# A mixed prompt and decode step: where the decode rows' attention takes its cached values from

## The chip, the cores and the metric

One core of one Trainium2 chip runs the whole program in one launch. The metric is the device time of that core in microseconds (us); of several runs the median is taken. The profile comes from one further execution of the same kernel.

## What is computed

A decoder trunk of two layers, all in float32, for a prompt of 512 tokens and for 8 sequences in decoding with 4 new tokens each (32 rows). Layer 0 is a convolution module and a SwiGLU feed-forward ("FFN0"). From its output one shared K/V is projected, and layer 1 attends with it in three branches (compressed, selected, window) and ends with a second feed-forward. For the decode rows the past 1024 tokens of the selected branch lie in a paged cache, and the page table says which page of 128 tokens is whose:

```python
def gather_pages(cache, page_table):
    g = cache[page_table]
    return g.reshape(page_table.shape[0], page_table.shape[1] * PAGE_SIZE, *cache.shape[2:])
...
sel_full = jnp.concatenate([gather_pages(cache_kv_sel, page_table), rows[:, :, 1]], axis=1)
...
blk_k, blk_v = selection_blocks(sel_full)
...
s_s = jnp.einsum('bqgrd,bgqksd->bgqksr', q, ks).astype(jnp.float32) + bias_s
p_s = masked_softmax(s_s.reshape(B, KV_HEADS, Q, nk, GROUP), smask.reshape(B, KV_HEADS, Q, nk)[..., None], 3)
o_s = jnp.einsum('bgqnr,bgqnd->bqgrd', p_s.astype(vs.dtype), vs.reshape(B, KV_HEADS, Q, nk, HEAD_DIM))
```

A token of `cache_kv_sel` is 2 KB: keys of 4 heads of 64 numbers (1 KB), then the values of the same heads (1 KB). `cache_kv_win` (512 past tokens a sequence) is laid out alike and not paged.

## The kernel before

The program is one stream of Python generators. TensorE (PE) does the matrix products, mostly as three passes over high and low halves of float32 numbers (`whi`, `wlo`, `h_hi`, `h_lo`, lines 183 and 185). The order of instructions on each engine is chosen at build time by a scheduler with a timing model of its own; on the chip every engine works through its own list strictly in order, and so do the DMA queues of SP (SyncE, where weights are loaded) and of POOL (GpSimd). Work with no hurry is handed to a long stage as `between` steps and is mixed into it.

Five pieces matter here:

- `setup` builds row tables from the page table: for each partition and sequence the row of the cache to fetch (`rows4`, four tables, lines 384 to 387).
- `key_steps` (lines 1289 to 1309) is mixed into FFN0. For each of 8 sequences and 3 chunks of 512 tokens (two of the paged cache, one of the window) it fetches the chunk into `kr`, transposes its keys on DVE (VectorE) into `ktr` (line 1304, two instructions a chunk) and writes them to a DRAM scratch `kt_d` with SP (line 1307, four writes). A paged chunk comes by one indirect DMA on POOL (`load_rows`, line 1030): 128 rows of 8 KB, each with four tokens' keys and values. The values half goes on to a second DRAM scratch, `v_d`, by one SP write of 512 KB (line 1299). `kr` has two buffers.
- `decode_attention(pool, gp)` (lines 1312 to 1461) runs for each of two pairs of heads, `gp`, and in it for two sets `st` of four sequences. Scores against the compressed keys (line 1324) and against `kt_d` (line 1379) go through the softmax (line 1346); the probabilities are transposed and multiplied with the values (line 1443, `b<-vs,pT`): for each chunk and sequence four products with 128 values each. Values stand in `vs` tiles, one per chunk and sequence, in 8 buffers. SP loads them from `v_d` (line 1434, 32 loads of 256 KB) and from the window cache (line 1436).
- `decode_rows` (lines 1182 to 1186) and `keys_values` (lines 1226 and 1231) write new rows out through POOL's DMA queue; `keys_values` is the projection of the prompt's shared K/V, and its products stand beside the decode attention on PE. `compressed_branch` (line 1558) stands behind them.
- `prompt_attention` comes next; its first product with probabilities is line 1530 (`o<-pTp,vn`). It takes over the PSUM banks that the decode attention used.

The values' way before, in lines 1299 and 1434:

```python
self.load_rows(kr.rearrange("p t e -> p (t e)"), A["cache_kv_sel"], 2 + c, b)
self.sy.dma_start(self.v_d[b, c].rearrange("(p t) d -> p t d", t=4), kr[:, :, 256:])
...
self.sy.dma_start(vb, self.v_d[bb[b], c].rearrange("(a p) d -> p a d", p=P)[:, :, gp * P:(gp + 1) * P])
```

Of the kernel before, what the change touches and what calls it, by code (L numbers as in the profile page):

```python
# [14 lines left out]
P = 128  # L15
# [3 lines left out]
NB = 8  # L19
# [45 lines left out]
def shape_constants():  # L65
# [22 lines left out]
    c["kbase"] = (p % 32).astype(f)[:, None]  # L88
    pages = np.arange(8)[:, None, None] == np.stack([p % 32 // 4, p // 32, 4 + p // 32])
    c["iota"] = np.broadcast_to(np.arange(16, dtype=f), (P, 16))  # L90
    names, cols, at = [], [], 0
# [22 lines left out]
class Kernel:  # L114
# [187 lines left out]
    def setup(self, sp):  # L302
# [46 lines left out]
        self.g.dma_start(ptab, A["page_table"].rearrange("b j -> j b"))  # L349
        ptf = sp.tile([8, NB], F32, name="ptf")  # L350

# [31 lines left out]
        for i in range(3):  # L383
            self.te.matmul(pt[:, i * NB:(i + 1) * NB], pages[:, i * P:(i + 1) * P], ptf, start=True, stop=True)
        for i, col in enumerate((self.cbase[:, 0:1], self.cbase[:, 1:2], self.kbase, self.kbase)):
            j = max(i - 1, 0)
            self.v.tensor_scalar(self.rows4[:, i], pt[:, j * NB:(j + 1) * NB], col, None, op0=ALU.add)
        pt = self.bank()
# [638 lines left out]
    def load_rows(self, out, cache, i, b):  # L1027

        src = cache.rearrange("n (k t) e g d -> (n k) (t e g d)", t=4)
        self.g.indirect_dma_start(out=out, out_offset=None, in_=src, in_offset=bass.IndirectOffsetOnAxis(ap=self.rows4[:, i, b:b + 1], axis=0))  # L1030

# [255 lines left out]


    def key_steps(self, pool):


        A = self.A
        winc = A["cache_kv_win"].rearrange("b (p t) e g d -> p b t (e g d)", t=4)
        for b in range(NB):
            for c in range(3):
                kr = pool.tile([P, 4, 512], F32, name="kr", bufs=2)
                if c < 2:
                    self.load_rows(kr.rearrange("p t e -> p (t e)"), A["cache_kv_sel"], 2 + c, b)
                    self.sy.dma_start(self.v_d[b, c].rearrange("(p t) d -> p t d", t=4), kr[:, :, 256:])
                else:  # L1300
                    self.sy.dma_start(kr[:, :, :256], winc[:, b, :, 0:256])
                kt = pool.tile([P, 2, 4, P], F32, name="ktr", bufs=2)
# [9 lines left out]
    def decode_attention(self, pool, gp):  # L1312
        A, v, s, g, te = self.A, self.v, self.s, self.g, self.te
        bs = pool.tile([P, SK], F32, name="bs1")
        self.sy.dma_start(bs, self.bs_d[gp].unsqueeze(0).broadcast_to([4, 32, SK]))
        winc = A["cache_kv_win"].rearrange("b (c p) e g d -> p b c (e g d)", p=P)
        for st in range(2):
            bb = range(4 * st, 4 * st + 4)
# [98 lines left out]
            for c in range(4):  # L1417
# [11 lines left out]
                if c < 3:  # L1429
                    vs = []  # L1430
                    for b in range(4):
                        vb = pool.tile([P, 4, P], F32, name="vs", bufs=8)
                        if c < 2:
                            self.sy.dma_start(vb, self.v_d[bb[b], c].rearrange("(a p) d -> p a d", p=P)[:, :, gp * P:(gp + 1) * P])
                        else:
                            self.sy.dma_start(vb, winc[:, bb[b], :, 256 + gp * P:256 + (gp + 1) * P])
                        vs.append(vb)
# [7 lines left out]

            od = pool.tile([P, 2, HD], F32, name="od", bufs=2)
            t0 = pool.tile([P, HD], F32, name="t0", bufs=1)
# [198 lines left out]
    def run(self):  # L1646
# [5 lines left out]
        with sbuf("const") as self.cp, sbuf("norm") as self.np, \  # L1652
# [9 lines left out]
            self.kt_d = dp.tile([NB, 3, 2, P, 512], F32, name="kt_d")  # L1662
            self.v_d = dp.tile([NB, 2, 512, 256], F32, name="v_d")
            self.vtail = dp.tile([NB, 40, 256], F32, name="vtail")
            self.rows4 = cp.tile([P, 4, NB], I32, name="rows4")
            self.cks = cp.tile([P, NB, 2, 32], F32, name="cks")
# [148 lines left out]
```

## Time and profile before

| what | value |
|---|---|
| time, median of 3 runs | 1660.17 us (1652.02 to 1661.15) |
| the profiled execution's own time | 1661.26 us |
| its span in the trace | 1659.5 us |
| PE (TensorE matmul) busy | 1555.0 us, 94% |
| DVE (VectorE) busy | 1107.8 us, 67% |
| ACT (ScalarE) busy | 694.1 us, 42% |
| POOL (GpSimd) busy | 235.2 us, 14% |
| DMA moved | 295.26 MB, mean 178 GB/s |

How to read it: times in the trace count from the start of the span. A busy PE counts its matmuls from start to modelled end. "Idle before" an instruction is the time its engine did nothing, put down to what ended it. A DMA's duration on POOL or SP is the time that it holds that queue's engine; when its bytes have landed is told apart. The DMA share of a stretch is the mean busy share of the core's 16 DMA engines.

### The profile page before, as it was taken

To read this page: it belongs to the slowest core of one execution; us is meant where nothing else is said; L and a number is where in the kernel's file an instruction comes from. 1 tells how busy PE (TensorE), PEld (TensorE's weight loads), DVE (VectorE), ACT (ScalarE), POOL (GpSimd) and SP (SyncE) were. 2 spreads that over 40 slices of the span, in tenths; PEclk is the share of its full clock that TensorE was granted. 3 is DMA by queue.
4 is the path that set the end of the run, shared out by engine and by line. 5 is a ranking of instruction groups with operands and counts; after the bars stand their busy time and mean duration, and the time that the engine had idled before them with its cause. 6 is when DMAs were issued, how large, how long until landed. Compare 5 with 4: busy or idle time off the path is not lost.

```text
span 1659.5 us, 31626 instructions
## 1 busy us (share of the span) xinstructions
PE 1555.0 (94%) x12423; PEld 1366.8 (82%) x12423; DVE 1107.8 (67%) x2369; ACT 694.1 (42%) x1443; POOL 235.2 (14%) x270
## 2 busy tenths in 40 slices
PE   6897998999988889999999899999999999999997
PEld 3784677989978878999977677655699999999997
DVE  2897866482447788576657644867856865874865
ACT  5321115242222344255445422755746542552554
POOL 3444401021220112001110000000011110110010
PEclk9898979999999999999999999999999999999999
DMA  9577575374399999834779895746122472333231
GB/s 307 140 200 155 151 241 168 117 227 130 112 241 312 299 303 325 247 103 106 184 228 306 245 282 183 237 148 229 52 68 73 152 233 84 91 114 90 79 91 64
DMA packets 315568, 295.26 MB, mean 178 GB/s; under 512 B 16019, under 2 KB 275485, under 8 KB 311179
## 3 DMA queue, kind: packets, MB, share of 16 engines
q1 hardware_dynamic: 304507, 237.24, 48.7%
q0 software_dynamic: 10224, 55.47, 10.7%
q8 instruction: 98, 1.61, 0.4%
q10 hardware_dynamic: 688, 0.53, 0.1%
q14 instruction: 51, 0.42, 0.1%
HBM read 256.28 MB, written 45.48 MB: 182 GB/s over the span
## 4 chain that ended last, share of the span: by engine, by line
PE 65%; DMA 13%; DVE 10%; issue 6%; SPq 2%; ACT 2%; POOL 1%; ACTq 0%; DVEq 0%; POOLq 0%
PE g L185 18%; PE g L183 17%; PE g L247 8%; DMA raw<-in_w_down_dram 4%; PE t L247 3%; PE t L155 3%; PE o L1530 2%; DMA raw<-in_w_ada_dram 2%; DVE wlo L196 2%; PE t L1049 2%; PE a L452 1%; PE t L1379 1%; PE t L730 1%; PE sc L1509 1%; DVE y L768 1%
## 5 line engine op out<-in xcount | busy, mean ns | idle before, releaser
L169 ACT CAST whi<-raw 128x512 fp32r<-128x512 f32 x250 | 149.7, 606 | 408.7 <-PE g L185 280.1
L170 DVE TENSOR_TENSOR wlo<-raw,whi 128x512 fp32r<-128x512 f32 x250 | 173.0, 696 | 156.5 <-ACT whi L169 155.6
L183 PE MATMUL g<-h_hi,whi 128*128 128x256 f32 (+1 forms) x584 | 170.5, 293 | 13.9 <-DVE un L680 9.3
L185 PE MATMUL g<-h_hi,whi 128*128 128x288 f32 (+4 forms) x584 | 173.5, 298 | 0.9 <-ACT h_hi L575 0.9
L185 PE MATMUL g<-h_hi,wlo 128*128 128x288 f32 (+4 forms) x584 | 173.9, 298 | 0.0
L185 PE MATMUL g<-h_lo,whi 128*128 128x288 f32 (+4 forms) x584 | 173.7, 297 | 0.0
L183 PE MATMUL g<-h_lo,whi 128*128 128x256 f32 (+1 forms) x584 | 168.3, 288 | 3.0 <-DVE h_lo L830 3.0
L183 PE MATMUL g<-h_hi,wlo 128*128 128x256 f32 (+1 forms) x584 | 167.3, 287 | 0.0
L183 PEld LDWEIGHTS g<-h_hi,whi 128*128 128x128 f32 x584 | 111.5, 191 | 27.3 <-issue 16.2
L247 PE MATMUL g<-T,whi 128*128 128x272 f32 x656 | 127.9, 291 | 4.1 <-DVE sg L261 2.5
L195 ACT CAST whi<-s 128x512 fp32r<-128x512 f32 x128 | 79.1, 620 | 99.9 <-PE g L247 61.7
L183 PE MATMUL g<-a_hi,whi 128*128 128x256 f32 (+1 forms) x372 | 108.0, 291 | 12.4 <-ACT ht L912 4.3
L183 PEld LDWEIGHTS g<-h_lo,whi 128*128 128x128 f32 x584 | 111.8, 192 | 8.0 <-issue 4.3
L185 PEld LDWEIGHTS g<-h_hi,whi 128*128 128x128 f32 x584 | 111.3, 191 | 4.2 <-issue 2.9
L185 PEld LDWEIGHTS g<-h_hi,wlo 128*128 128x128 f32 x584 | 111.3, 191 | 2.6 <-issue 2.5
L185 PEld LDWEIGHTS g<-h_lo,whi 128*128 128x128 f32 x584 | 111.2, 190 | 2.6 <-issue 2.5
L183 PEld LDWEIGHTS g<-h_hi,wlo 128*128 128x128 f32 x584 | 111.5, 191 | 1.8 <-issue 1.7
L196 DVE TENSOR_TENSOR wlo<-s,whi 128x512 fp32r<-128x512 f32 x128 | 89.1, 698 | 34.0 <-ACT whi L195 32.2
L185 PE MATMUL g<-a_hi,wlo 128*128 128x288 f32 (+1 forms) x372 | 111.1, 299 | 0.0
L185 PE MATMUL g<-a_hi,whi 128*128 128x288 f32 (+1 forms) x372 | 110.9, 299 | 0.0
L185 PE MATMUL g<-a_lo,whi 128*128 128x288 f32 (+1 forms) x372 | 110.7, 298 | 0.0
L247 PEld LDWEIGHTS g<-T,whi 128*128 128x128 f32 x656 | 103.8, 190 | 5.6 <-ACT whi L195 2.2
(511 smaller groups left out, 4165.2 us busy)
## 6 DMA issues: line engine op xcount, KB each, us to landing
raw<-in_w_ada_dram SPq DMA_DIRECT2D x84, 512.0 KB
raw<-in_w_gate_dram SPq DMA_DIRECT2D x44, 512.0 KB
raw<-in_w_up_dram SPq DMA_DIRECT2D x44, 512.0 KB
raw<-in_w_down_dram SPq DMA_DIRECT2D x32, 512.0 KB
raw<-in_w_pw_dram SPq DMA_DIRECT2D x24, 512.0 KB
kt_d<-ktr SPq DMA_DIRECT2D x96, 128.0 KB
kt<-kt_d SPq DMA_DIRECT2D x24, 512.0 KB
raw<-in_w_kv_dram SPq DMA_DIRECT2D x20, 512.0 KB
```

Source lines behind the costliest of these rows:

```text
L155: self.te.transpose(out, in_, self.ident[:n, :n])
L169: self.s.copy(hi[:, :b - a], raw[:, a:b])
L170: self.v.tensor_tensor(out=lo[:, :b - a], in0=raw[:, a:b], in1=hi[:, :b - a].bitcast(F32), op=ALU.subtract)
L183: self.te.matmul(pg[:, 0, :split], a, b[:, i, :split], start=st, stop=sp)
L185: self.te.matmul(pg[:, 1, :tokens - split], a, b[:, i, split:tokens], start=st, stop=sp)
L195: self.s.copy(hi, src)
L196: self.v.tensor_tensor(out=lo, in0=src, in1=hi.bitcast(F32), op=ALU.subtract)
L247: self.te.matmul(out, a[:, i], b(i), start=first and i == 0 and j == 0, stop=i == 3 and j == 2, skip_group_check=not first)
L452: self.te.matmul(pa[32 * j:32 * j + 32, :256], self.cT[:, k, :], w[:, j * 256:(j + 1) * 256], start=k == 0, stop=k == KT - 1)
L730: self.te.matmul(pt[32 * gg:32 * gg + 32], wds[q // 4][:, gg, q % 4], vs[:, gg, 4 * q:4 * q + cols], start=q == 0, stop=q == 7)
L1049: te.matmul(ph[:, :P], self.w1[:, e, c // 2, c % 2], xv[:, c % 2, c // 2], start=c == 0, stop=c == 15)
L1530: te.matmul(po[rp * HD:(rp + 1) * HD, :256], self.vn[:, br, t, gg * HD:(gg + 1) * HD], pT[:, rp * 256:(rp + 1) * 256], start=br == 0 and t ...
```

## The change

The values are no longer fetched with the keys, nor kept in `v_d`, which is gone.

- In `key_steps` a paged chunk comes by four indirect DMAs in place of one, each with 128 rows of 1 KB: the keys of one token per partition. The table `rowsk` (four small DVE instructions) holds their rows. `kr` is half as large and has four buffers. The write to `v_d` is dropped.
- In `decode_attention` each `vs` tile of a paged chunk is filled by four indirect DMAs on POOL, each with 128 rows of 512 B (the values of one token for one pair of heads): 64 for each `gp`, 128 in all, in place of 32 loads on SP. Their table `rowsv` is made for each `gp` by eight small products with the page table and one DVE instruction. `od` has one buffer in place of two.
- `rows4` shrinks to two tables; `rowk` and the page table in float32 (`ptf`) stay in SBUF. One more transposition of `vb` into a bank of its own stands in `setup`; nothing reads it.

```diff
@@ setup
-        for i, col in enumerate((self.cbase[:, 0:1], self.cbase[:, 1:2], self.kbase, self.kbase)):
-            j = max(i - 1, 0)
-            self.v.tensor_scalar(self.rows4[:, i], pt[:, j * NB:(j + 1) * NB], col, None, op0=ALU.add)
+        for i in range(2):
+            self.v.tensor_scalar(self.rows4[:, i], pt[:, :NB], self.cbase[:, i:i + 1], None, op0=ALU.add)
+        self.v.tensor_scalar(self.rowk.rearrange("p c b -> p (c b)"), pt[:, NB:3 * NB], self.kbase, None, op0=ALU.add)
+        pt = self.bank()
+        self.transpose(pt[:, :66], vb)
@@ 
+    def gather(self, out, rows, at):
+        self.g.indirect_dma_start(out=out, out_offset=None, in_=rows, in_offset=bass.IndirectOffsetOnAxis(ap=at, axis=0))
@@ key_steps
+        rows = pool.tile([P, 4, 2, NB], I32, name="rowsk")
+        for t in range(4):
+            self.v.tensor_scalar(rows[:, t], self.rowk, 8.0, 2.0 * t, op0=ALU.mult, op1=ALU.add)
         for b in range(NB):
             for c in range(3):
-                kr = pool.tile([P, 4, 512], F32, name="kr", bufs=2)
+                kr = pool.tile([P, 4, 256], F32, name="kr", bufs=4)
                 if c < 2:
-                    self.load_rows(kr.rearrange("p t e -> p (t e)"), A["cache_kv_sel"], 2 + c, b)
-                    self.sy.dma_start(self.v_d[b, c].rearrange("(p t) d -> p t d", t=4), kr[:, :, 256:])
+                    for t in range(4):
+                        self.gather(kr[:, t], A["cache_kv_sel"].rearrange("n t e g d -> (n t e) (g d)"), rows[:, t, c, b:b + 1])
                 else:
-                    self.sy.dma_start(kr[:, :, :256], winc[:, b, :, 0:256])
+                    self.sy.dma_start(kr, winc[:, b, :, 0:256])
@@ decode_attention
+        pt = self.bank("ds")
+        for j in range(8):
+            te.matmul(pt[:, j * NB:(j + 1) * NB], self.ident[:8, j:j + 1].broadcast_to([8, P]), self.ptf, start=True, stop=True)
+        rows = pool.tile([P, 8, NB], I32, name="rowsv")
+        v.tensor_scalar(rows.rearrange("p j b -> p (j b)"), pt[:, :8 * NB], self.vrow[:, 0:1], self.vrow[:, gp + 1:gp + 2], op0=ALU.mult, op1=ALU.add)
...
                         if c < 2:
-                            self.sy.dma_start(vb, self.v_d[bb[b], c].rearrange("(a p) d -> p a d", p=P)[:, :, gp * P:(gp + 1) * P])
+                            for j in range(4):
+                                self.gather(vb[:, j], A["cache_kv_sel"].rearrange("n t e (h g) d -> (n t e h) (g d)", h=2),
+                                            rows[:, 4 * c + j, bb[b]:bb[b] + 1])
...
-            od = pool.tile([P, 2, HD], F32, name="od", bufs=2)
+            od = pool.tile([P, 2, HD], F32, name="od", bufs=1)
@@ run
-            self.v_d = dp.tile([NB, 2, 512, 256], F32, name="v_d")
```

The build-time order moves with it, at three places. The first is POOL's list while the keys are fetched (`kr` are the keys, `a_lo` the low half of an FFN0 activation that PE reads), before:

```order
L1030 DMA kr<-in_cache_kv_sel_dram,rows_78 128x2048 x2
L920 TENSOR_TENSOR a_lo<-ht,a_hi 128x544
L1030 DMA kr<-in_cache_kv_sel_dram,rows_78 128x2048
L920 TENSOR_TENSOR a_lo<-ht,a_hi 128x544
L1030 DMA kr<-in_cache_kv_sel_dram,rows_78 128x2048 x7
L984 TENSOR_TENSOR a_lo<-ht,a_hi 128x544
```

and after:

```order
L1037 DMA kr<-in_cache_kv_sel_dram,rowsk 128x256 x12
L924 TENSOR_TENSOR a_lo<-ht,a_hi 128x544
L1037 DMA kr<-in_cache_kv_sel_dram,rowsk 128x256 x12
L924 TENSOR_TENSOR a_lo<-ht,a_hi 128x544
L1037 DMA kr<-in_cache_kv_sel_dram,rowsk 128x256 x40
L988 TENSOR_TENSOR a_lo<-ht,a_hi 128x544
```

Twelve gathers stand where two and one stood, and all 64 come before the third `a_lo` shown here; before, six of the 16 came behind it.

The second place is POOL's list in the decode attention (`vs` are the value gathers, `rows` the decode rows written out, `row`, `vn` and `acc` the rows that `keys_values` writes out). Before it holds no `vs`:

```order
L1164 TENSOR_TENSOR hs<-hs,rstd 128x256
L1182 DMA out_dram<-rows 32x256
L1184 DMA out_dram<-rows 4x256 x8
L1182 DMA out_dram<-rows 32x256
L1184 DMA out_dram<-rows 4x256 x8
L1186 DMA vtail<-rows 8x4x256 x2
L1226 DMA out_dram<-row 128x4x256 x2
L1231 DMA out_dram<-acc 32x512
L1226 DMA out_dram<-row 128x4x256
L1226 DMA out_dram<-vn 128x4x256
L1226 DMA out_dram<-row 128x4x256
L1226 DMA out_dram<-vn 128x4x256
```

and after, from the last write of the decode rows on (15 gathers stand ahead of the first of these writes):

```order
L1193 DMA vtail<-rows 8x4x256 x2
L1037 DMA vs<-in_cache_kv_sel_dram,rowsv 128x128 x17
L1233 DMA out_dram<-row 128x4x256
L1037 DMA vs<-in_cache_kv_sel_dram,rowsv 128x128 x32
L1233 DMA out_dram<-row 128x4x256
L1238 DMA out_dram<-acc 32x512
L1037 DMA vs<-in_cache_kv_sel_dram,rowsv 128x128 x32
L1233 DMA out_dram<-row 128x4x256
L1233 DMA out_dram<-vn 128x4x256
L1037 DMA vs<-in_cache_kv_sel_dram,rowsv 128x128 x32
L1233 DMA out_dram<-row 128x4x256
L1233 DMA out_dram<-vn 128x4x256
```

The 128 gathers come as 15, 17, 32, 32 and 32, with the 20 writes of the decode rows behind the first 15, and one or two of the writes of `keys_values` between the later groups; one `row` and one `vn` stand just ahead of the last 32.

The third place is PE's list at the end of the decode attention (`vs,pT` are the products with the values, `g<-` those of `keys_values`, `ht,zk` those of the compressed branch). Before, the last values are followed by 288 passes `g<-` ahead of line 1530:

```order
L1443 MATMUL b<-vs,pT 32x128 x14
L1443 MATMUL b<-vt,pT 32x128 x4
L183 MATMUL g<-h_hi,whi 128x256
L185 MATMUL g<-h_hi,whi 128x256
L183 MATMUL g<-h_lo,whi 128x256
```

and after by 96:

```order
L1461 MATMUL b<-vs,pT 32x128 x16
L157 MATMUL a<-c_small,tl 40x128
L1461 MATMUL b<-vs,pT 32x128 x32
L1461 MATMUL b<-vt,pT 32x128 x4
L157 MATMUL b<-c_small,od 128x128
L1576 MATMUL b<-ht,zk 32x512 x4
```

So 192 passes of `keys_values` moved ahead of the last products with values; the compressed branch's eight products stand behind them in both.

## Rows read from the trace of the kernel before

**Rows 1.** the page's first lines: busy time, share and instructions of each engine

```profile
PE 1555.0 (94%) x12423; PEld 1366.8 (82%) x12423; DVE 1107.8 (67%) x2369; ACT 694.1 (42%) x1443; POOL 235.2 (14%) x270
```

**Rows 2.** windows: length, busy us (count) of PE, PEld, DVE, ACT, POOL, PEclk, DMA share, GB/s

```profile
460.00:660.00 200.00, 176.72 (x1336) 164.36 (x1335) 146.29 (x244) 70.65 (x137) 30.53 (x27) 0.95 0.99 298
...
580.00:620.00 40.00, 35.05 (x264) 31.80 (x263) 32.66 (x53) 16.68 (x33) 6.11 (x5) 0.96 1.00 304
620.00:660.00 40.00, 36.53 (x286) 32.79 (x285) 34.93 (x57) 19.49 (x39) 8.51 (x7) 1.00 1.00 317
...
780.00:820.00 40.00, 35.71 (x280) 34.96 (x279) 23.82 (x58) 19.76 (x40) 6.17 (x12) 1.00 0.85 188
...
820.00:1060.00 240.00, 229.49 (x2037) 181.60 (x2036) 142.15 (x438) 101.38 (x231) 17.62 (x31) 0.99 0.81 243
```

**Rows 3.** DMA of the stretch 460 to 700 us

```profile
DMA packets 80561, 70.78 MB, mean 295 GB/s; under 512 B 3368, under 2 KB 76034, under 8 KB 78493
```

**Rows 4.** line 1304, the key transpositions on DVE: ns min/median/max, first and last start

```profile
L1304 DVE STREAM_TRANSPOSE ktr<-kr x48: 1053/1094/1147, 482.5 to 684.4; 128x512 f32<-128x512 f32 x48
```

**Rows 5.** POOL in order of time, at the first key gathers

```profile
473.32 1.05 POOL L1030 DMA_INDIRECT kr<-in_cache_kv_sel_dram,rows  x1 [11.97 <-DMA line_f<-lsb]
474.67 0.97 POOL L1030 DMA_INDIRECT kr<-in_cache_kv_sel_dram,rows  x1 [0.30 <-issue]
475.67 1.36 POOL L920 TENSOR_TENSOR a_lo<-ht,a_hi 128x544 fp32r<-128x544 f32 x1
```

**Rows 6.** PE's instructions on tile a_lo, 470 to 510 us

```profile
L183 PE MATMUL g<-a_lo,whi x16: 275/282/415, 486.8 to 509.8; 128*128 128x256 f32 x16
```

**Rows 7.** the chain of waits, 780 to 1080 us: start, us, what

```profile
785.83 19.34 DMA raw<-in_w_down_dram
```

**Rows 8.** SP in order of time, 780 to 812 us

```profile
786.24 19.76 SPq L1434 DMA_DIRECT2D vs<-v_d  x6
```

**Rows 9.** line 1030, the gathers on POOL

```profile
L1030 POOL DMA_INDIRECT kr<-in_cache_kv_sel_dram,rows x16: 936/973/1468, 473.3 to 658.3; - x16
...
DMA to landing us min/median/max: 5.6/8.5/10.6
```

**Rows 10.** line 1324, the first products of the decode attention

```profile
L1324 PE MATMUL t<-cks,qz x32: 196/206/217, 856.1 to 946.5; 128*32 128x32 f32 x32
```

**Rows 11.** POOL in order of time, 820 to 1060 us

```profile
863.49 0.57 POOL L1182 DMA_DIRECT2D out_dram<-rows  x1 [32.91 <-ACT rows L1175]
...
875.44 1.18 POOL L1186 DMA_DIRECT2D vtail<-rows  x2
930.19 0.81 POOL L1226 DMA_DIRECT2D out_dram<-row  x1 [53.57 <-ACT row L132]
...
988.09 0.79 POOL L1226 DMA_DIRECT2D out_dram<-row  x1 [24.65 <-DVE row L134]
1006.22 0.75 POOL L1226 DMA_DIRECT2D out_dram<-vn  x1 [17.34 <-DVE vn L134]
```

**Rows 12.** line 1443, the products with the values, and what PE waited for there

```profile
L1443 PE MATMUL b<-vs,pT x384: 272/273/421, 885.5 to 988.0; 128*32 128x128 f32 x192
L1443 PE MATMUL b<-vt,pT x32: 269/281/293, 900.8 to 988.3; 40*32 40x128 f32 x32
...
  DMA vs<-in_cache_kv_win_dram: 1.2, 3
```

**Rows 13.** the chain of waits: one batch of 34 products with values

```profile
987.18 1.41 PE b L1443 x34
```

**Rows 14.** line 1530, the prompt attention's products with probabilities

```profile
L1530 PE MATMUL o<-pTp,vn x320: 379/379/431, 1048.5 to 1218.3; 128*64 128x256 f32 x160
```

**Rows 15.** PE in order of time, two passes of keys_values

```profile
1002.34 0.28 PE L183 MATMUL g<-h_hi,whi 128*128 128x256 f32 x1
1002.46 0.28 PE L185 MATMUL g<-h_hi,whi 128*128 128x256 f32 x1
```

**Rows 16.** plain DMAs on POOL, mean duration

```profile
L1184 POOL DMA_DIRECT2D out_dram<-rows x16 | 8.2, 519 | 2.6 <-DMA out_dram<-rows 2.4
```

More of the change, by code (lines that the diff above doesn't have):

```diff
@@ L89, in shape_constants @@
     pages = np.arange(8)[:, None, None] == np.stack([p % 32 // 4, p // 32, 4 + p // 32])
+    c["vrow"] = np.stack([512 + 0 * p, 4 * p + 2, 4 * p + 3], 1).astype(f)
     c["iota"] = np.broadcast_to(np.arange(16, dtype=f), (P, 16))
@@ L349, in setup @@
         self.g.dma_start(ptab, A["page_table"].rearrange("b j -> j b"))
-        ptf = sp.tile([8, NB], F32, name="ptf")
+        ptf = self.ptf
         self.s.activation(c9, c9, AF.Silu)
@@ L1029, in load_rows @@
         src = cache.rearrange("n (k t) e g d -> (n k) (t e g d)", t=4)
-        self.g.indirect_dma_start(out=out, out_offset=None, in_=src, in_offset=bass.IndirectOffsetOnAxis(ap=self.rows4[:, i, b:b + 1], axis=0))
+        self.gather(out, src, self.rows4[:, i, b:b + 1])
+    def gather(self, out, rows, at):
+        self.g.indirect_dma_start(out=out, out_offset=None, in_=rows, in_offset=bass.IndirectOffsetOnAxis(ap=at, axis=0))
     def compress_steps(self, pool):
@@ L1662, in run @@
             self.kt_d = dp.tile([NB, 3, 2, P, 512], F32, name="kt_d")
-            self.v_d = dp.tile([NB, 2, 512, 256], F32, name="v_d")
             self.vtail = dp.tile([NB, 40, 256], F32, name="vtail")
-            self.rows4 = cp.tile([P, 4, NB], I32, name="rows4")
+            self.rows4 = cp.tile([P, 2, NB], I32, name="rows4")
+            self.rowk = cp.tile([P, 2, NB], F32, name="rowk")
+            self.ptf = cp.tile([8, NB], F32, name="ptf")
             self.cks = cp.tile([P, NB, 2, 32], F32, name="cks")
```

## The prediction

> **What bounds the kernel now.** I read the page's busy times first. PE is busy 94% of the span, POOL 14% [rows 1]: POOL has room on average, but an average says nothing of one stage. So the second view is busy time by windows [rows 2]. Two stretches matter. From 460 to 660 us the keys are fetched beside FFN0: PE is busy 176.72 of 200 us at a mean granted clock of 0.95, and the DMA share stands at 0.99. That stretch is held back by transfers, by 200 - 176.72 = 23.3 us at most, and by the clock as well. From 820 to 1060 us (decode rows, decode attention, projection of the shared K/V) PE is busy 229.49 of 240 us, so PE is the bound there, and POOL is busy just 17.62 us. The wait list of the value products shows PE waiting three times, 1.2 us in all, for values of the window and not for those of the scratch [rows 12]: the loads that the change takes away cost PE nothing there. The third view is the chain of waits. Just before, at 785.83, it runs for 19.34 us through a load of `w_down` [rows 7], while SP's list shows six early value loads issued right behind it over 19.76 us [rows 8]; PE loses 40 - 35.71 = 4.3 us in that window [rows 2].
>
> **The change, part by part.**
>
> *Fetching keys: a gain.* The gathers shrink from 16 x 128 x 8 KB = 16.8 MB to 64 x 128 x 1 KB = 8.4 MB, and the writes to `v_d`, 16 x 512 KB = 8.4 MB, go. That is 16.8 of the 70.78 MB that move from 460 to 700 us [rows 3], 24%. It isn't 24% of the time: PE can get back only its idle time. Moreover the new order draws the key transpositions together: where they stood in 48 places from 482.5 to 684.4 us [rows 4], all 64 gathers now stand ahead of an `a_lo` that had six of 16 behind it. The first part of the stretch therefore stays full of transfers and the last part becomes free. I take PE's idle time of the last two windows, 40 - 35.05 and 40 - 36.53, together 8.4 us [rows 2].
>
> Against that, POOL's list puts 12 gathers ahead of the `a_lo` that stood behind two. A gather holds POOL 0.973 us in the median [rows 9], and 0.30 us passes before the next [rows 5]: **1.27 us each**. From 473.32 the 12 end at 488.6, `a_lo` with its 1.36 us at 490.0 [rows 5]; PE first reads it at 486.8 [rows 6]. Cost 3.2 us. The six early loads of values vanish from SP, so I count the 4.3 us at 785 as gained. **Lead** when the decode attention starts: 8.4 + 4.3 - 3.2 = 9.5 us. Its ends: all idle time and the clock back is 23.3 + 4.3 + 5% of 176.72, 36 us; with gathers at 1.77 us (the longest, 1.468, and the gap) the `a_lo` would be some 10 us late and nothing gained, -10 us.
>
> *Fetching values: a loss.* 128 gathers now stand in POOL's list, where none was. The trace has none with rows of 512 B. The nearest row is the key gather: also 128 rows, on the same queue, but 16 times the bytes. From below I bound it by a plain DMA on POOL, 0.52 us [rows 16], from above by 1.77 us. I take 1.27 us, since number of rows and kind of instruction agree and only the bytes differ. Row and gap show that gathers are not run one after another: the second started 1.35 us behind the first [rows 5], though one takes 8.5 us until its data has landed [rows 9].
>
> The Trainium skill, "DMA: Bandwidth & Descriptors", section "Anatomy of one DMA", fits a DMA from this queue by 2.0 us plus bytes over 436 GB/s, which is 2.15 us for 64 KB (an estimate from the page); one after the other, 128 would hold the queue 275 us, and the sum below would be near 1790 us. By the two rows just given the fixed part overlaps, so the trace speaks against adding it up.
>
> Now the queue, step by step. The index table hangs on products that stand just ahead of line 1324, which started at 856.1 [rows 10]; less the lead, 846.6. Fifteen gathers: 865.7. The decode rows' 20 writes hold POOL from 863.49 to 876.62 [rows 11], 13.1 us: 878.8. Seventeen gathers: 900.4. One `row`, 0.81: 901.2. Thirty-two: 941.8. Two small writes, 1.6: 943.4. Thirty-two: 984.1; `row`, 0.8: 984.9. Next stands `vn`, and it isn't ready: it was at 1006.22 [rows 11], so 996.7 now, and what is queued behind it, the last 32 gathers, waits 12 us with it. With its 0.75 us: 997.5. Thirty-two gathers: 1038.1. The last, issued at 1036.8, lands 8.5 us later: 1045.3. Its 36 products take 1.5 us, as 34 took 1.41 [rows 13]: **1046.8**, where the last one before ended at 988.6 [rows 12]. So the values, which SP had ready in time, become the last thing to arrive, by 58 us. The eight buffers of `vs` hold 32 gathers, 41 us of the queue, so they don't add a wait.
>
> *What PE does meanwhile.* PE isn't idle for 58 us: 192 passes of `keys_values` moved ahead of the last value products. At 0.12 us a pass (1002.34 to 1002.46) [rows 15] that is 23.0 us of work no longer behind them. Before, 1048.5 - 988.3 = 60.2 us lay between the last value product and the prompt attention's first product with probabilities [rows 12, 14]; now 60.2 - 23.0 = 37.2 us, since the compressed branch and the remaining passes still stand behind and the prompt attention takes over the banks. It comes at 1046.8 + 37.2 = 1084.0, 35.5 us late.
>
> *The small edits* cost nothing that counts: the index tables, 16 products of eight columns and six DVE instructions in all, and the dead transposition are under a microsecond each and lie beside transfers; without that cover they would add some 3 us. `od` with one buffer is reused tens of microseconds later. Transposing keys costs the same 48 x 1094 ns [rows 4].
>
> **Sum.** The profiled execution took 1661.26 us, 1.1 above the median. 1661.26 + 35.5 = 1696.8; against the median of 1660.17, **1696 us**. From 1084 us on nothing is changed.
>
> **Rivals.**
>
> *Faster.* One mechanism: gathers whose price goes with their bytes. If one holds POOL for 0.52 us, as a plain small DMA does, the queue reaches `vn` early and only the last group counts: 997.5 + 32 x 0.52 = 1014.1, landing after 5.6 [rows 9], less the last issue: 1019.2, products 1020.7, plus 37.2 = 1057.9, or 9.4 us late with my lead. With the whole lead of 36 us it is 17 us early: 1643 us. For it speaks that the trace shows only gathers of 1 MB; against it, that their duration barely varies from 936 to 973 ns [rows 9], like a fixed price. It decides from 0.72 us a gather down with the whole lead: then the 32 behind `vn` are done soon enough to come out over 0.5% below. 6%.
>
> *No difference.* Either half of that: cheap gathers with my lead, 1670 us, or gathers of 1.27 us with the whole lead, 35.5 - 26.9 = 8.6 us, 1669 us; and between them. A tenth. Half a percent, 8.3 us, is what a measurement of this kernel can tell from no change. 10%.
>
> *Much slower.* Gathers stretched by other engines. The longest key gather took 1.468 us [rows 9], half as much again as the median. At 1.77 us each the queue runs to 1032.8 ahead of `vn`, no wait there, 1090 behind the last group, landing 10.6 us after issue, 1137.7 for the prompt attention: 89 us late, 1750 us. Against it: the key gathers ran beside a DVE that was busy 146.29 of 200 us, and in the decode attention it is less busy, 142.15 of 240 [rows 2]. The Trainium skill, "SBUF — State Buffer", has a "DVE blocks DMA" trap, 620 ns alone against 3100 ns beside a DVE copy, and by it this case would be worse still; the median of 973 ns bears it out for few gathers at most. 16%.
>
> *The change doesn't do what it says:* the order shows all 128 gathers on POOL and no `v_d`, so I give that no chance of its own.
>
> **How the numbers follow.** The forecast, gathers of 1.1 to 1.5 us and a lead of 0 to 20 us, has 68%. The range runs from 1667, where the no-difference cases lie, to 1736, short of the much slower case; it leaves out the faster 6% and most of the 16%. Faster 0.06, same 0.10, slower 0.84.
>
> **What would show it.** In the profile after: POOL busy some 200 us more, value gathers near 1 us each and 1.3 us apart; the last key transposition tens of microseconds earlier and less PE idle from 580 to 660; POOL waiting for `vn` ahead of the last 32 gathers; last value product near 1047; PE waiting for `vs` from the cache. I am wrong if the gathers take much less than a microsecond, if PE shows no wait for `vs`, or if the prompt attention starts before 1060.

## The result, and the profile after

| | before | after |
|---|---|---|
| time, median | 1659.78 us of 4 runs (1652.02 to 1661.15) | **1716.35 us** of 4 runs (1713.23 to 1723.7) |
| ratio of the runs, 95% interval | | **1.0344** [1.0314, 1.0375] |
| the profiled execution | 1661.26 us, span 1659.5 | 1716.69 us, span 1714.9 |

The change makes the kernel 3.4% slower. The forecast was 1696 us, from 1667 to 1736: sign, place and mechanism held, and the loss came out larger than the sum. Below it is taken apart on the profiled execution.

First the page's busy times of the kernel after, to be held against [rows 1]:

```profile
PE 1577.5 (92%) x12456; PEld 1375.5 (80%) x12456; DVE 1109.7 (65%) x2374; ACT 695.3 (41%) x1443; POOL 408.5 (24%) x446
```

POOL has 176 instructions and 173.3 us more. PE's work is the same but for 33 small matmuls (32 of them make the index tables, 0.12 us apart, so some 4 us in all), and yet it is busy 22.5 us longer: for the rest, matmuls at a lower granted clock take longer. Where, the windows show (columns as in [rows 2]):

```profile
460.00:660.00 200.00, 178.14 (x1390) 165.34 (x1389) 158.25 (x253) 72.83 (x141) 80.29 (x73) 0.97 0.85 251
580.00:620.00 40.00, 36.19 (x279) 33.57 (x279) 35.61 (x56) 20.06 (x41) 4.99 (x3) 1.00 0.66 181
620.00:660.00 40.00, 38.22 (x313) 34.30 (x313) 24.82 (x42) 17.42 (x33) 6.07 (x4) 1.00 0.57 172
780.00:820.00 40.00, 40.00 (x320) 39.82 (x319) 26.89 (x64) 20.33 (x43) 6.17 (x13) 1.00 0.57 139
820.00:1060.00 240.00, 191.88 (x1703) 149.07 (x1701) 106.70 (x323) 75.30 (x156) 141.36 (x153) 0.87 0.68 205
1020.00:1060.00 40.00, 14.11 (x115) 6.49 (x111) 3.01 (x13) 2.40 (x10) 27.36 (x29) 0.50 0.27 78
1060.00:1100.00 40.00, 33.90 (x173) 20.23 (x172) 17.93 (x52) 12.03 (x31) 1.59 (x2) 0.81 0.56 171
```

The key stage has room now (DMA share 0.85 instead of 0.99). PE is busy just 1.4 us more in it, but does 54 matmuls more in the same 200 us (1390 for 1336), at a clock of 0.97 instead of 0.95: busy time alone doesn't tell how far it got. From 820 to 1060 us PE is idle 48.1 us instead of 10.5, at a mean clock of 0.87 instead of 0.99. The worst slice is 1020 to 1060: PE busy 14.11 of 40 us and a granted clock of 0.50, the lower level, 1.2 GHz; POOL is the busiest engine of that slice. From 1060 to 1100 the clock is still 0.81 on the mean.

The cause stands in POOL's list of the same stretch, in order of time (rows of gathers without a wait left out), beside [rows 11]:

```profile
845.57 1.04 POOL L1037 DMA_INDIRECT vs<-in_cache_kv_sel_dram,rowsv  x1 [27.23 <-DVE mx L1356]
...
865.37 0.57 POOL L1189 DMA_DIRECT2D out_dram<-rows  x1
...
878.68 1.19 POOL L1193 DMA_DIRECT2D vtail<-rows  x2
...
911.01 0.82 POOL L1233 DMA_DIRECT2D out_dram<-row  x1 [7.57 <-ACT row L134]
926.39 0.98 POOL L1037 DMA_INDIRECT vs<-in_cache_kv_sel_dram,rowsv  x1 [14.56 <-PE b L1461]
...
967.14 0.81 POOL L1233 DMA_DIRECT2D out_dram<-row  x1
...
973.49 1.01 POOL L1037 DMA_INDIRECT vs<-in_cache_kv_sel_dram,rowsv  x1 [4.99 <-issue]
...
1014.43 0.82 POOL L1233 DMA_DIRECT2D out_dram<-row  x1
1015.24 0.80 POOL L1233 DMA_DIRECT2D out_dram<-vn  x1
```

The queue's first item goes out at 845.57, its last at 1055.22. Three waits in it are of some 5 us or more: for a `row` that isn't ready (7.57), for a buffer that PE's products have to free (14.56), and for the second index table (4.99; it is one buffer, so it can be made only when the first pair's 64 gathers are through). `vn` no longer waits. The gathers as a group (line 1037), with the last row the time from issue to landing of the value gathers alone (the view of `vs`):

```profile
L1037 POOL DMA_INDIRECT vs<-in_cache_kv_sel_dram,rowsv x128: 940/945/1465, 845.6 to 1055.2; - x128
...
L1037 POOL DMA_INDIRECT kr<-in_cache_kv_sel_dram,rowsk x64: 942/949/1518, 458.8 to 571.4; - x64
...
DMA to landing us min/median/max: 2.4/5.6/7.0
```

Rows of 512 B (945 ns) cost POOL what rows of 1 KB cost (949) and rows of 8 KB before (973, [rows 9]): a price for the instruction, not for the bytes. Who waits for them is told by the products with values (line 1461), to be held against [rows 12]:

```profile
L1461 PE MATMUL b<-vs,pT x384: 272/297/423, 877.5 to 1059.6; 128*32 128x128 f32 x192
...
L1461 PE MATMUL b<-vt,pT x32: 269/355/420, 928.4 to 1060.2; 40*32 40x128 f32 x32
...
  DMA vs<-in_cache_kv_sel_dram,rowsv: 70.2, 36
```

The last row adds up matmuls and weight loads, which wait together; the matmuls alone wait 31.7 us, 18 times, and before for nothing from the scratch. The chain of waits ends in the queue:

```profile
1055.22 2.46 DMA vs<-in_cache_kv_sel_dram,rowsv
1057.72 2.97 PE b L1461 x42
```

And the first product of the prompt attention with probabilities, against 1048.5 in [rows 14]:

```profile
L1548 PE MATMUL o<-pTp,vn x320: 379/379/689, 1102.9 to 1273.7; 128*64 128x256 f32 x160
```

That is 54.4 us late. From there to the end of the span it is 612.0 us, before 611.0: next to nothing else is lost. The loss lies wholly between 820 and 1103 us.

### The profile page after: what moved, and what is told of

Its sections match the earlier page's. It is cut to its first block, busy times and chain, and to the rows that moved or that the text cites. A ratio compares the mean times of both kernels' runs of the same rounds, so it can differ in the third digit from the quotient of the medians.

```text
span 1714.9 us, 31924 instructions
## 1 busy us (share of the span) xinstructions
PE 1577.5 (92%) x12456; PEld 1375.5 (80%) x12456; DVE 1109.7 (65%) x2374; ACT 695.3 (41%) x1443; POOL 408.5 (24%) x446
## 5 line engine op out<-in xcount | busy, mean ns | idle before, releaser
L172 DVE TENSOR_TENSOR wlo<-raw,whi 128x512 fp32r<-128x512 f32 x250 | 177.8, 713 | 147.8 <-ACT whi L171 143.9
L1037 POOL DMA_INDIRECT vs<-in_cache_kv_sel_dram,rowsv x128 | 127.0, 992 | 85.0 <-issue 37.0
```

The source lines that it names most:

```text
L172: self.v.tensor_tensor(out=lo[:, :b - a], in0=raw[:, a:b], in1=hi[:, :b - a].bitcast(F32), op=ALU.subtract)
L1037: self.g.indirect_dma_start(out=out, out_offset=None, in_=rows, in_offset=bass.IndirectOffsetOnAxis(ap=at, axis=0))
```

## The experiments

Twelve kernels ran; each ratio is against runs of the kernel before on the same chip. The table gives the stage marks of each profile: the decode attention's first product (`t<-cks,qz`), the last value product (`b<-vs,pT`), and the prompt attention's first product with probabilities.

| kernel | median us | ratio, 95% interval | first `cks` | last `vs` | first `pTp` |
|---|---|---|---|---|---|
| before (rows above) | | | 856.1 | 988.0 | 1048.5 |
| after | 1716.35 | 1.0344 [1.0314, 1.0375] | 844.7 | 1059.6 | 1102.9 |
| keys_alone | 1665.12 | 1.0025 [0.9995, 1.0054] | 854.1 | 989.5 | 1051.5 |
| values_alone | 1811.23 | 1.0871 [1.0801, 1.0941] | 850.9 | 1163.8 | 1205.9 |
| half_gathers | 1710.66 | 1.0306 [1.0259, 1.0352] | 858.0 | 1031.2 | 1097.3 |
| pages_on_sp | 1716.36 | 1.0307 [1.0256, 1.0357] | 867.4 | 1045.0 | 1106.9 |
| rows_on_sp | 1715.85 | 1.0324 [1.0286, 1.0363] | 848.1 | 1061.9 | 1104.7 |
| half_rows_on_sp | 1670.01 | 1.0052 [1.0025, 1.0079] | 846.6 | 986.5 | 1052.8 |
| early_tables | 1693.44 | 1.0179 [1.0137, 1.022] | 853.0 | 1043.9 | 1084.1 |
| early_rows_on_sp | 1699.91 | 1.0235 [1.0188, 1.0282] | 852.9 | 1046.0 | 1089.0 |
| pages_on_pool | 1696.53 | 1.0191 [1.0155, 1.0227] | 862.8 | 1045.9 | 1086.0 |
| pages_pool_rows_sp | 1696.81 | 1.0223 [1.0194, 1.0253] | 858.5 | 1039.2 | 1080.5 |
| before_late_values | 1659.56 | 0.9977 [0.9951, 1.0003] | 852.8 | 988.6 | 1049.2 |
| keys_alone_late_values | 1657.43 | 0.9973 [0.995, 0.9996] | 847.4 | 979.0 | 1039.7 |

Each edit is scheduled anew at build time, so the order of PE's list isn't held fixed. Six kernels (keys_alone, half_gathers, half_rows_on_sp, pages_on_sp and the two late_values) have 288 passes `g<-` between the last value product and the prompt attention, as before has; the other six have 96, as after. With 288 the times run from 1657 to 1716 us, with 96 from 1693 to 1811, so this order alone doesn't set the time. But no run has 128 gathers in the order of before, so what part of the loss is the order's was not separated.

### One half of the change alone

**keys_alone**: the new key gathers; the values by 32 loads of SP from fixed pages, without the index tables, so it leaves out the lookup of the values' pages.

```diff
-                            for j in range(4):
-                                self.gather(vb[:, j], ..., rows[:, 4 * c + j, bb[b]:bb[b] + 1])
+                            at = 8 * bb[b] + 4 * c
+                            self.sy.dma_start(vb, A["cache_kv_sel"][at:at + 4].rearrange("a p e g d -> p a (e g d)")[:, :, 256 + gp * P:256 + (gp + 1) * P])
```

> The keys' part of the change alone: keys by single tokens, no scratch for the values; SP loads the values in 32 transfers of 256 KB (rows of 512 B) straight from fixed pages of the cache, so the lookup of the values' pages is left out. Theory (POOL's queue of 128 gathers is the whole loss, the keys' part is a gain): the first score product of the decode attention stays near 845 us as in the changed kernel (856 before), the last value product comes near 977, the time is 1644 to 1652 us. Rival D (rows of 512 B from the cache are slow for the DMA engines whoever issues them): over 1690 us. Rival K (single-token key gathers gain nothing): 1660 us or more.

Measured: 1665.12 us, ratio 1.0025 [0.9995, 1.0054]. The loss is gone, so it belongs to the value gathers, with the order of PE's list that is built around them; rival D falls. There is no gain either, as rival K had said, and all three numbers of the theory were missed. The lead at `cks` is 2.0 us, not 8 or more; its chain of waits still has the load that stood in [rows 7]:

```profile
784.12 18.88 DMA raw<-in_w_down_dram
```

**values_alone**: the keys as before (16 gathers of 1 MB, two buffers, without the write to `v_d`), the 128 value gathers as after.

```diff
-                kr = pool.tile([P, 4, 256], F32, name="kr", bufs=4)
+                kr = pool.tile([P, 4, 512], F32, name="kr", bufs=2)
...
-                    for t in range(4):
-                        self.gather(kr[:, t], ...)
+                    self.load_rows(kr.rearrange("p t e -> p (t e)"), A["cache_kv_sel"], 2 + c, b)
```

> The values' part alone: keys by gathers of 1 MB as before, without the write to the scratch; the values by 128 gathers on POOL. Theory: 1716 to 1728 us, up to 11 us over the changed kernel, as the lead of the keys' part shrinks but not wholly (the 16 writes of 512 KB are still gone); gathers 1.25 us apart; last value product 1060 to 1070. Rival D: the same. Rival K (the keys' part costs time): below 1710 us.

Measured: 1811.23 us, far beyond what either theory gave. It agrees with the value gathers as the costly half, but it can't be added to keys_alone: the two don't give the whole. What more it showed stands in the last section.

### How many gathers, and what stands between them

**half_gathers**: 64 value gathers instead of 128, and for the window's values four buffers of their own. It leaves out half of the values and uses the other half twice.

```diff
-                                for j in range(4):
+                                for j in range(2):
...
-                        vb = pool.tile([P, 4, P], F32, name="vs", bufs=8)
+                        vb = pool.tile([P, 2 if c < 2 else 4, P], F32, name="vs" if c < 2 else "vw", bufs=8 if c < 2 else 4)
```

> The changed kernel with two of the four gathers of each chunk and sequence; their values are used twice, so half of the values are left out, and the window's values have four buffers of their own. 64 value gathers instead of 128. Theory (serial queue): 64 x 1.25 = 80 us and the 20 writes end before 950 us, ahead of the projection's products, so nearly the whole loss goes: 1645 to 1665 us. If the loss were proportional to gathers or bytes (rival D): half of it, near 1685 us.

Measured: 1710.66 us. By the price alone 64 gathers less are 80 us less queue, and next to nothing came of it. Not because of the queue: no value product waits for a gather here. These are the largest entries among PE's waits from 820 to 1110 us (us in total, times, longest):

```profile
PE b L1461 <- issue: 9.5, 10, 3.6
PE g L185 <- DVE acc L136: 6.5, 1, 6.5
PE g L185 <- issue: 5.2, 6, 1.5
PE t L1404 <- issue: 4.7, 5, 1.9
```

"issue" is waiting for which the profile names nothing. It makes 25.1 us in 32 pieces here, and none in the kernel after. Besides, the decode attention began 13.3 us later than in after (858.0 for 844.7). So the time decides neither for the theory nor for the rival. POOL's list in order of time shows where POOL waited:

```profile
902.54 0.98 POOL L1037 DMA_INDIRECT vs<-in_cache_kv_sel_dram,rowsv  x1 [11.18 <-PE b L1461]
...
948.80 1.00 POOL L1037 DMA_INDIRECT vs<-in_cache_kv_sel_dram,rowsv  x1 [17.63 <-PE t L1395]
...
968.52 0.84 POOL L1233 DMA_DIRECT2D out_dram<-row  x1
990.13 0.98 POOL L1037 DMA_INDIRECT vs<-in_cache_kv_sel_dram,rowsv  x1 [20.78 <-PE b L1461]
```

Here POOL waits for PE to free buffers, and the first `row` stands behind those gathers: it goes out at 968.52, where it went at 930.19 [rows 11]. `keys_values` has one `row` tile and can't refill it until it is written out, and passes of it stand in PE's list ahead of later value products. That the two hold each other up was the next theory; it is argued from the lists, and no wait of PE's matmuls here hangs on a `row`.

**rows_on_sp** and **half_rows_on_sp** put the seven writes of `keys_values` on SP's queue, in the kernel after and in half_gathers.

```diff
-                    g.dma_start(po[:, :, e * 256:(e + 1) * 256], row)
+                    self.sy.dma_start(po[:, :, e * 256:(e + 1) * 256], row)
```

> The changed kernel with the rows that the projection of the shared K/V writes out (seven DMAs) issued by SP instead of POOL. Theory A (length of the queue alone): the 128 gathers still take 160 us from 845 us on, time 1700 to 1716 us. Theory B (gathers and row writes block each other in POOL's one list: writes stand behind gathers that wait for buffers which PE frees, and the projection has a single row tile): the 7.6 us wait ahead of the first row write and some of the 14.6 us behind it go, last gather near 1035 instead of 1055 us, time 1680 to 1700 us. Rival C (it is PE's order that was fixed at build time, whatever the queues do): 1716 us.

> Half of the value gathers (as in half_gathers, two tokens' values used twice) and the projection's row writes on SP. Theory B: with neither a long queue nor writes behind gathers the time comes down to that of keys_alone, 1655 to 1680 us. Theory A says nothing here, since half_gathers alone stayed at 1710 us. Rival C: 1700 us or more.

Measured: 1715.85 and 1670.01 us. With 64 gathers the same edit gives 40.7 us, with 128 nothing. In half_rows_on_sp the gathers still wait for PE, but nobody waits behind them, and the last value product comes at 986.5. In rows_on_sp the waits only move: POOL's list has

```profile
928.65 0.94 POOL L1037 DMA_INDIRECT vs<-in_cache_kv_sel_dram,rowsv  x1 [21.73 <-PE b L1461]
```

where after had 7.57 and 14.56 us apart, 22.1 together. So with 128 gathers the writes in POOL's list don't set the time: theory A's range and rival C's number held, theory B's fell. What the 40.7 us with 64 gathers are isn't shown. In the profiled executions 11.4 us lie ahead of the decode attention (846.6 for 858.0), where both kernels run the same lists on every engine, and half_gathers has its 25.1 us of waits without a name, half_rows_on_sp none. Both also gave the window its own buffers, so against the kernel after number and buffers can't be told apart.

### When the queue starts

**early_tables** makes both index tables ahead of the queries, so that the first gather needn't wait for the decode attention; **early_rows_on_sp** has the writes on SP as well.

```diff
+                    self.rowsv = dpool.tile([P, 2, 8, NB], I32, name="rowsv")
+                    for gp in range(2):
+                        self.v.tensor_scalar(self.rowsv[:, gp].rearrange("p j b -> p (j b)"), pt[:, :8 * NB], self.vrow[:, 0:1], self.vrow[:, gp + 1:gp + 2], op0=ALU.mult, op1=ALU.add)
```

> The changed kernel with both index tables of the values made before the queries, in one tile of their own, so that the gathers can start when the pool opens (near 820 us instead of 845) and the second table does not wait for the first 64 gathers (5 us). Theory A: the whole queue moves 25 to 30 us ahead, 1685 to 1695 us. Theory B: the eight buffers hold back all but the first 32 gathers, which still wait for PE: 1690 to 1716 us. Rival C: 1716 us.

> Both edits: tables made early, and the projection's row writes on SP. Theory A: as early_tables, 1685 to 1695 us. Theory B: below either edit alone, 1660 to 1685 us. Rival C: 1716 us.

Measured: 1693.44 and 1699.91 us. POOL's list of early_tables:

```profile
829.81 1.04 POOL L1037 DMA_INDIRECT vs<-in_cache_kv_sel_dram,rowsv  x1 [4.37 <-DVE rowsv L1755]
...
890.91 1.11 POOL L1037 DMA_INDIRECT vs<-in_cache_kv_sel_dram,rowsv  x1 [5.42 <-PE b L1456]
...
952.60 0.98 POOL L1037 DMA_INDIRECT vs<-in_cache_kv_sel_dram,rowsv  x1 [17.96 <-PE b L1456]
```

The queue starts 15.8 us earlier and sends its last item 20.6 us earlier (1034.6), PE's matmuls wait 13.6 us for gathers instead of 31.7, the last value product comes 15.7 us earlier, and the time falls by 22.9 us. When the queue starts counts, then, as theory A says, and rival C's 1716 us are missed. But 1693.44 lies in B's range too, the 25 to 30 us weren't reached, and POOL waits 24.0 us for buffers, as B had it. From 1026 on the chain of waits runs over PE again, whose last value product comes 9.3 us behind the last gather. That the block alone is the cause is refuted by early_rows_on_sp, which was to gain and lost 6.5 us to early_tables; it lies above theory A's range as well.

### The same bytes without an indirect gather

**pages_on_sp** and **pages_on_pool** replace each value gather by a plain transfer of 64 KB whose page comes from a register, on SP's and on POOL's queue; **pages_pool_rows_sp** is the latter with the writes of `keys_values` on SP.

```diff
-                                self.gather(vb[:, j], ..., rows[:, 4 * c + j, bb[b]:bb[b] + 1])
+                                page = self.nc.values_load(self.pti[bb[b]:bb[b] + 1, 4 * c + j:4 * c + j + 1], engines=[mybir.EngineType.SP], ...)
+                                self.sy.dma_start(vb[:, j], A["cache_kv_sel"][bass.ds(page, 1)].rearrange("a p e g d -> (a p) (e g d)")[:, 256 + gp * P:256 + (gp + 1) * P])
```

> The changed kernel with the values' 128 transfers of 64 KB issued by SP, the page number read from the page table into a register for each (a page is 128 tokens in one piece, so no list of rows is needed). Complete computation. Theory (the loss is POOL's queue): 1643 to 1660 us, below the kernel before if 128 issues and register loads take SP under 1 us each. Rival D: over 1690 us. A rival of its own: register loads of 2 us and more hold up SP's weight loads, over 1665 us.

> The changed kernel with the 128 value gathers replaced by 128 plain transfers of 64 KB that POOL issues itself, each with its page from a register (no index table, so the queue needn't wait for it). Computation complete. Theory A (the queue's length is what counts: number of items times the price of one): an item costs 0.8 to 0.9 us as it did on SP, 128 of them about 110 us in place of 160, and the first eight buffers are filled before the decode attention starts; last product with values 1010 to 1035, 1665 to 1695 us. Rival B (the wait for buffers that PE frees and the writes of keys_values behind it set the end, whatever an item costs): POOL waits 20 us or more for buffers, last product later than 1040, 1700 to 1720 us. Third: the load of a page number into a register costs POOL over 1 us, an item 2 us or more, and the time is above 1740 us.

> pages_on_pool with the seven writes of keys_values moved from POOL's queue to SP's. Computation complete. In pages_on_pool POOL waited 54.1 us in four stretches for buffers that PE's value products free, and the writes of keys_values stood behind those transfers. Theory B (the two block each other in one list, and what is lost beyond the queue's price is that): keys_values runs on while POOL waits, PE idles at least 15 us less from 900 to 1060, last product with values before 1030, 1665 to 1685 us. Rival W (32 transfers a set of four sequences against eight buffers is what holds PE back: POOL can fetch the next set only when PE has used the last one, wherever the rows are written): POOL waits 45 us or more for PE's products again, 1690 to 1702 us, as rows_on_sp stood to the changed kernel.

Measured: 1716.36, 1696.53 and 1696.81 us. For pages_on_sp rival D's number came true, but not for its reason: keys_alone brings the same rows of 512 B by SP without loss. On SP an item costs about 0.85 us, but what SP has to bring besides now stands behind them. SP's list of pages_on_sp (line 1449 are the values):

```profile
906.26 10.99 SPq L1449 DMA_DIRECT2D vs<-in_cache_kv_sel_dram  x13
...
918.44 13.47 SPq L1449 DMA_DIRECT2D vs<-in_cache_kv_sel_dram  x16
932.01 1.34 SPq L1146 DMA_DIRECT2D q_d<-qst  x3
933.41 0.65 SPq L1326 DMA_DIRECT2D bs<-bs_d  x1
```

`bs`, the bias of the next scores, is issued at 933.41, in the kernel after at 897.68, and DVE waits 15.2 us for it. Part of the loss lies ahead: the decode attention begins 11.3 us later than before (867.4 for 856.1). On POOL an item costs 0.94 us and needs no index table, so 32 of them are through before the decode attention starts. What POOL then waited for (pages_on_pool, line 1449, us and times):

```profile
  PE b L1458: 54.1, 4
```

and in pages_pool_rows_sp:

```profile
  PE b L1458: 63.8, 6
```

Theory A came near with the price, 0.94 us for 0.8 to 0.9, and with the time, 1696.53 for 1665 to 1695, but the last product came at 1045.9 and not by 1035; rival B had the waits and the late product, and not the time. With the writes moved, W held and B fell: POOL waits as long, and nothing is gained. A set of four sequences needs eight tiles from the cache and four of the window, twelve for eight buffers, so the queue can't fetch the next set until PE has used the last one; then 32 items at 0.94 us are 30 us, with 1.29 us they are 41, beside the at most 34 us that PE took from one set to the next before ((988.0 - 885.5) / 3, [rows 12]). That reading is argued from the buffers and the waits; more buffers for the whole computation weren't tried, so how much of the some 36 us that remain is theirs stays open.

### Where the lead came from

**before_late_values** is the kernel before, with the loads from `v_d` held back behind the decode rows' first load of `w_kv`; **keys_alone_late_values** has the same edit on keys_alone.

```diff
+                            with self.tc.issue_after(self.first_kv):
+                                self.sy.dma_start(vb, self.v_d[bb[b], c]...)
```

> The kernel before with one edit: SP may issue the 32 value loads from the scratch only behind the first load of the decode rows' w_kv; its list then holds none of them ahead of the last w_down load, where six stood. Computation complete. Theory L (the 11.4 us by which the decode attention starts earlier in the changed kernel come from the early value loads that are absent there, and not from the smaller key gathers): the first product with cks moves from 856.1 to 844 to 848, PE busy 39 to 40 of 40 us in 780 to 820, and the time is 1647 to 1656 us, 0.3 to 0.8% under before. Rival K (the lead comes from the key stage): cks stays at 853 to 857, 1658 to 1664 us. Second rival (the loads only collide later, with the w_kv and query loads): PE full in 780 to 820, but PE idle 5 us or more longer in 820 to 860, and 1657 to 1668 us.

> keys_alone with the same one edit (its 32 value loads from fixed cache pages only behind the first w_kv load); the page lookup of the values is left out, so their time alone counts. Theory L: cks at 842 to 847, and the same gain of 8 to 11 us over keys_alone: 1652 to 1658 us, level with before_late_values within 5 us, since the keys' part is worth nothing. Rival K: nothing gained over keys_alone, 1660 to 1668 us, and cks near 854.

Measured: 1659.56 us, ratio 0.9977 [0.9951, 1.0003], and 1657.43 us, 0.9973 [0.995, 0.9996]. The lead at `cks` is 3.3 us by the late loads alone, 2.0 by the keys alone, 8.7 by both, and 11.4 in the kernel after, which has no such loads at all. By the times K holds for the first and L for the second. But each lead is that of one execution, and executions differ by as much. Up to 779 us after and half_gathers run the same lists on every engine; the last product `a<-raw,cT`, behind the key stage, started in after and in half_gathers at

```profile
L456 PE MATMUL a<-raw,cT x464: 379/379/637, 26.4 to 720.7; 128*32 128x256 f32 x155
L456 PE MATMUL a<-raw,cT x464: 379/379/636, 27.6 to 731.9; 128*32 128x256 f32 x155
```

With the same lists up to there it came at 728.0 in keys_alone and 722.7 in keys_alone_late_values, with those of before at 729.5 in before and 728.3 in before_late_values. So where the lead came from isn't shown. And it doesn't reach the end in before_late_values: DVE waits there for `bs`, whose data it gets at 923.4 us, before at 923.0 (DVE's waits, 890 to 945 us),

```profile
DVE pc L1342 <- DMA bs<-bs_d: 8.3, 1, 8.3
```

against 4.4 us in the kernel before, and at the prompt attention before_late_values is 0.7 us behind before. With the smaller keys as well the prompt attention starts 8.8 us earlier, but the median is only 0.3% below before. No complete kernel here beats the kernel before by more than a measurement can tell.

## Why the prediction was right, and by how much it missed

It forecast a loss of 35.5 us up to the prompt attention, and 54.4 were measured. Of the 18.9 us between them, 13.4 lie ahead of the last product with values (1060.2 for 1046.8) and 5.5 behind it.

- **The place: right.** PE was the bound from 820 to 1060 and became the one that waits; the values, in time before, became the last thing to arrive.
- **The price of a gather: right.** 1.27 us was taken; leaving out the waits and the other writes, the five groups took 165.0 us, 1.29 each, and 1.25 where none was stretched. So both rivals on the price fall: a cheap gather (0.72 us or less) by the 945 ns, a stretched one (1.77 us) by the mean and by a longest of 1465 ns among 128. The Trainium skill, "DMA: Bandwidth & Descriptors", section "Anatomy of one DMA", gives 2.15 us for 64 KB (an estimate from its fit); the trace agrees with about that as the shortest time to landing, 2.4 us, and not as the distance of two gathers, 1.25 us: the fixed part overlaps, as the two rows before had suggested. The trap of DVE against DMA that the Trainium skill has ("SBUF — State Buffer", section "A bandwidth-pool intuition that's wrong (but worth ruling out)") stretches a DMA from 620 to 3100 ns; no value gather of the kernel after held POOL longer than 1465 ns, so it doesn't show there.
- **"The eight buffers of `vs` hold 32 gathers ... so they don't add a wait": wrong.** This is the step that failed, with two more waits that were put at nothing. The window's four tiles of a set use the same eight buffers, and POOL waits 14.56 us for one of them. It waits 4.99 us for the second index table, and 7.57 for the first `row`: the sum lets that go at 901.2 as if it were ready, though by the rule that it uses for `vn` it would come at 930.19 - 9.5 = 920.7 [rows 11]. In place of 12 us for `vn`, which didn't occur, came 7.57 + 14.56 + 4.99 = 27.1 us; that a wait which didn't come made up for half of those that did is luck. With the stretched gathers (2.5 us) and slower writes of the decode rows (1.4), less a start 1.0 us earlier, that gives 18.0 of the 18.4 us by which the last gather was late (1055.22 for 1036.8).
- **Landing: too long.** 8.5 us was the median of 1 MB gathers; the last of 64 KB landed in 2.46 us. It gave back 6.0 us, and 42 products at the lowered clock took 2.97 us for the 1.5 counted.
- **Behind the last product: 42.7 us for 37.2.** The right passes had moved, but the clock was left out: granted 0.50 while PE waited, and 0.81 in the slice behind.
- **The lead: 11.4 for 9.5, near by number and not shown by cause.** The first product after:

```profile
L1340 PE MATMUL t<-cks,qz x32: 192/196/218, 844.7 to 951.4; 128*32 128x32 f32 x32
```

  The bytes went (54.49 MB from 460 to 700 us for 70.78, [rows 3]), the last key transposition came 91.5 us earlier, and PE does 42 matmuls more in the last two windows. Whether that is the term of 8.4 us can't be told: with the same lists up to there, executions stood 11.2 us apart behind the key stage (the two rows of `a<-raw,cT` above), and keys_alone brought no gain. The `a_lo` that was to be ready at 490.0 was ready at 478.5, for the gathers started at 458.82 and not at 473.32, and PE read it 7.2 us earlier than before (479.6 for 486.8, [rows 6]). In the window at 785 PE is busy its 4.3 us more, 40.00 for 35.71; from `a<-raw,cT` (720.7 for 729.5) to `cks` the lead grows by 2.6.
- **"No difference" and "faster"** needed cheap gathers or a lead of 36 us; neither showed. POOL's extra 173 us for the "some 200" and PE's waits for `vs` were as forecast; the wait ahead of the last 32 gathers was not.

## What to carry to other kernels

Price a gather by its number of instructions and not by its bytes, and read its queue as a schedule: when it can start, what stands between its items, and whose buffers it waits for. A transfer that was early because nothing hung on it becomes the bound when it is moved behind the moment that needs it, and work that shares its list (here the writes of `row`) is held up with it. Before the time of an experiment is held against a theory, look in its trace whether it lost its time in the place that the theory is about: half_gathers didn't, and a lead of some 10 us in one profile is no more than executions of the same list differ by.

## What was not expected

In values_alone PE stood still for no reason that the profile names. Its waits from 820 to 1170 us (us in total, times, longest):

```profile
PE g L187 <- issue: 20.7, 16, 3.8
PE g L185 <- issue: 17.2, 19, 2.4
...
PE b L1457 <- issue: 7.0, 12, 1.7
...
PE t L1391 <- issue: 5.0, 4, 1.8
PE a L157 <- issue: 3.8, 2, 3.6
```

That is 53.7 us in 53 pieces. In order of time it looks like this:

```profile
990.35 0.40 PE L187 MATMUL g<-h_hi,whi 128*128 128x288 f32 x1 [2.43 <-issue]
993.15 0.37 PE L185 MATMUL g<-h_lo,whi 128*128 128x256 f32 x1 [2.40 <-issue]
995.95 0.40 PE L187 MATMUL g<-h_lo,whi 128*128 128x288 f32 x1 [2.42 <-issue]
997.35 0.37 PE L185 MATMUL g<-h_hi,wlo 128*128 128x256 f32 x1 [1.00 <-issue]
998.05 0.40 PE L187 MATMUL g<-h_hi,wlo 128*128 128x288 f32 x1 [0.33 <-issue]
```

Matmuls start 2.8, 1.4 and 0.7 us apart with nothing to wait for, while POOL issues gathers back to back (954 to 994 us). half_gathers has 25 us of the same, while before, after and the other ten kernels have none in this stretch, some with as many gathers. What slows PE's issuing there stays open, and so do the 95 us by which values_alone is slower than the whole change: the 53.7 us are part of them.
